# Eight chunks of the second feed-forward product as seven block products

## The chip, the cores and the metric

The kernel runs on one core of a Trainium2 chip, in one launch. The metric is device time in microseconds (us). The kernel before takes 1285.72 us, the median of three runs (1285.38 to 1285.79).

## The reference, cut to what matters

A trunk of four residual layers works on 256 tokens of 1024 channels, in float32. In each layer a token mixer is followed by a SwiGLU feed-forward block with 2816 hidden channels; only the second product of that block is touched here.

```
for i in range(4):
    x = x + concat([mix, mo]) @ w_o[i]                   # mixer and memory attention
    gu = rmsnorm(x, g_ffn[i]) @ w_ffn_in[i]              # 1024 -> 2 * 2816
    h = silu(gu[:, :2816]) * gu[:, 2816:]                # hidden, 256 x 2816
    x = x + h @ w_ffn_out[i]                             # 2816 -> 1024
out = rmsnorm(x, g_final)
```

## The kernel before, in words

All products run on TensorE (PE) in a reduced 32-bit form. Each operand is split into a high part and a low rest, and one 128 x 128 block of the left side meets 512 columns of the right in three matmuls: high by high, high by low, low by high (`mm3`, L136 to L138). A weight chunk comes by DMA from the SP queue into a tile `raw` (8 buffers); ScalarE (ACT) casts it to `whi` (L131) and VectorE (DVE) subtracts to get `wlo` (L132), 1024 elements per partition in one instruction. `whi` and `wlo` have 8 buffers each, so the splitting can run up to eight chunks ahead of PE.

`proj` forms 512 columns for two tiles of 128 tokens over the 1024 inputs. `strassen` forms 1024 columns (a left and a right half) in seven block products in place of eight: the tokens are halved (two tiles of 128), the inputs are halved (4 chunks of 128), the columns are halved. Each product has two steps `s` of two chunks, that is two times six matmuls (L214 to L216). The sums of weight blocks (`wsum`, and `raw` added in place; 8 adds of 1024 elements) are made on DVE at L224, and each of the 14 weight operands is split as any chunk is. The token sides are made once per layer by `tokens_side` (names `sh`, `sl`). The products share four PSUM banks: products 1 and 2; 5 and 3; 7 and 4; and 6. Between them stand `su = acc[6] + sv` and `sy = acc[7] + su` (L224): product 4 adds into the bank of product 7, so its first matmul waits until `sy` has read it. `strassen` is used before the change for column blocks b = 1 and b = 4 of the first feed-forward product; the use at b = 4 is called the first block product below.

The hidden values come out in six column blocks b (five of 512, one of 256). `h_out` or `gated` scales and gates them, and `hidden` transposes them on PE (L864), casts to `hh` on ACT (L867) and subtracts to `hl` on DVE (L868); block 5 uses one tile `hb`. These are the left sides of the second product.

`out_proj` forms that second product. It holds four PSUM banks (two token tiles by two column halves) over all 22 chunks of 128 hidden channels, 12 matmuls to a chunk; the last four chunks are held back and worked off bank by bank, so that the residual add (`residual`, L826), the transposes and the norm of the next layer start while PE still works.

The order of each engine's instructions is set by a scheduler when the kernel is built; each engine then takes its own list strictly in order. `later` and `flush` put off the transposes by some rounds. Tiles named `tag="att"` share 11 buffers, those of `big` share 12, and PSUM has 8 banks.

Of the kernel before, what the change touches and what calls it, by code (L numbers as in the profile page):

```python
# [9 lines left out]
F32 = mybir.dt.float32  # L10
F32R = mybir.dt.float32r
BF16 = mybir.dt.bfloat16
AF = mybir.ActivationFunctionType
ALU = mybir.AluOpType
# [3 lines left out]
P = 128  # L18
# [3 lines left out]
DEPTH = 4  # L22
# [4 lines left out]
NFF = DFF // P  # L27
# [5 lines left out]
NATT = 11  # L33


V_MIX, V_FFN, V_MEM, V_HEAD, V_CONV = 0, 32, 64, 72, 74
# [4 lines left out]
def trunk_kernel(ctx, tc, x, mem, vecs, w_in, w_kv, w_o, w_f1, w_f2, lams, g_final, out):  # L41
    nc = tc.nc
# [4 lines left out]
    big = pool("big", 12)  # L47
    xtp = pool("xtp", 2)
    work = pool("work", 2)
# [17 lines left out]
    xs = []  # L67
# [48 lines left out]
    def wchunk(srcs, nk, ncol, ahead=False):  # L116
        if ahead:
            raw = big.tile([P, nk, ncol], F32, name="raw", tag="big")
        else:
            raw = wraw.tile([P, nk, ncol], F32, name="raw", tag="raw")  # L120
        c = 0
        for s in srcs:
            n = s.shape[1]
            nc.sync.dma_start(raw[:, :, c:c + n], s.rearrange("(c p) n -> p c n", p=P))
            c += n
        return wparts(raw, nk, ncol)

    def wparts(raw, nk=2, ncol=512):
        hi = wsplit.tile([P, nk, ncol], F32R, name="whi", tag="whi")
        lo = wsplit.tile([P, nk, ncol], F32R, name="wlo", tag="wlo")  # L130
        nc.scalar.copy(hi, raw)  # L131
        wlast[:] = [nc.vector.tensor_tensor(lo, raw, hi.bitcast(F32), ALU.subtract)]  # L132
        return hi, lo

    def mm3(ps, lh, ll, wh, wl, first, last):
        nc.tensor.matmul(ps, lh, wh, start=first, stop=False)  # L136
        nc.tensor.matmul(ps, lh, wl, start=False, stop=False)  # L137
        return nc.tensor.matmul(ps, ll, wh, start=False, stop=last)  # L138
# [4 lines left out]
    def later(rounds, f):  # L143
        pend.append([rounds, f])
# [117 lines left out]
    def negative(rs):  # L262
# [3 lines left out]
            nc.vector.tensor_scalar(out[-1], r, -1.0, None, ALU.mult)  # L266
        return out

    def tokens_side(xg, xT):

        a11, a12, a21, a22 = xg[0][0], xg[0][1], xg[1][0], xg[1][1]
        half = lambda t, h: tuple(x[:, 4 * h:4 * h + 4, :] for x in xT[t])
        ab = {1: half(0, 0), 2: half(0, 1), 4: half(1, 1)}
        tt, stt = nc.vector.tensor_tensor, nc.vector.scalar_tensor_tensor

        def parts(src):
            hi = work.tile([P, 4, P], F32R, name="sh", tag="att", bufs=NATT)
            lo = work.tile([P, 4, P], F32R, name="sl", tag="att", bufs=NATT)
            nc.scalar.copy(hi, src)
            tt(lo, src, hi.bitcast(F32), ALU.subtract)  # L280
            return hi, lo

        tt(a22, a22, a21, ALU.subtract)
        ab[5] = parts(a22)
        tt(a21, a11, a21, ALU.subtract)
        ab[7] = parts(a21)
        stt(a11, a22, -1.0, a11, ALU.mult, ALU.subtract)
        ab[6] = parts(a11)
        stt(a12, a12, -1.0, a11, ALU.mult, ALU.subtract)
        ab[3] = parts(a12)  # L290
        return ab

    def out_proj(w, order, lhs, lag, evac, settle=None):

        acc = [[ps_acc.tile([P, 512], F32, name="acc", tag="ps") for _ in range(2)] for _ in range(NT)]
        chunks = [2 * kp + k for kp in order for k in range(2)]
        n = len(chunks)

        def mms(t, h, j, ch):
            lh, ll = lhs(chunks[j], t)  # L300
            sl = slice(h * 512, (h + 1) * 512)
            mm3(acc[t][h], lh, ll, ch[0][:, 0, sl], ch[1][:, 0, sl], j == 0, j == n - 1)

        tail = []
        for j, kc in enumerate(chunks):
            ch = wchunk([w[kc * P:(kc + 1) * P, :]], 1, D)
            if j < n - 2 * lag:
                for t in range(NT):
                    for h in range(2):
                        mms(t, h, j, ch)  # L310
                flush()
            else:
                tail.append((j, ch))
        if settle is not None:
            settle()
        for t in range(NT):
            for h in range(2):
                for j, ch in tail:
                    mms(t, h, j, ch)
                flush()  # L320
                evac(t, h, acc[t][h])
# [383 lines left out]
    for i in range(DEPTH):  # L705
# [117 lines left out]
        def residual(gcol, nxt, rnx, keep=None):  # L823
            def evac(t, h, acc):
                sl = slice(h * 512, (h + 1) * 512)
                nc.vector.tensor_tensor(xs[t][:, sl], acc, xs[t][:, sl], ALU.add)  # L826
                if h == 0:
                    nxt.append(xt_tiles())
                    if keep is not None:
                        keep.append([])  # L830
                later(1, lambda: transposed(nxt[t], xs[t], gcol, h, None if keep is None else keep[t]))
                if h == 1:
                    rnx.append(stats(xs[t]))
            return evac

        nxt, rnx, xg = [], [], []
# [2 lines left out]


        hts = []
        for b in range(6):
            n = 512 if b < 5 else 256
            if n == 512:
                hh = big.tile([P, 4, S], F32R, name="hh", tag="big")
                hl = big.tile([P, 4, S], F32R, name="hl", tag="big")
            else:
                both = big.tile([P, 2, 2, S], F32R, name="hb", tag="big")
                hh, hl = both[:, 0], both[:, 1]
            hts.append((hh, hl))  # L850
            sg = [work.tile([P, 512], F32, name="sg", tag="qkn", bufs=4) for _ in range(NT)]

            def h_out(t, g_ps, u_ps, hh=hh, hl=hl, sg=sg, n=n):
                s = sg[t][:, :n]
                if g_ps is not None:
                    nc.scalar.activation(s, g_ps, AF.Silu, scale=rx[t])
                if u_ps is not None:
                    nc.vector.scalar_tensor_tensor(s, u_ps, rx[t], s, ALU.mult, ALU.mult)
                    later(1, lambda: hidden(t, s, hh, hl, n))

            def hidden(t, s, hh, hl, n):
                tr = ps_x.tile([P, 4, P], F32, name="tr", tag="ps")
                for c in range(n // P):
                    nc.tensor.transpose(tr[:, c, :], s[:, c * P:(c + 1) * P], ident)  # L864
                src = tr[:, :n // P, :]
                hi = hh[:, :, t * P:(t + 1) * P]
                nc.scalar.copy(hi, src)  # L867
                nc.vector.tensor_tensor(hl[:, :, t * P:(t + 1) * P], src, hi.bitcast(F32), ALU.subtract)  # L868

            c0 = b * 512  # L870
            gcols, ucols = w_f1[i, :, c0:c0 + n], w_f1[i, :, DFF + c0:DFF + c0 + n]
            if b in (1, 4):
                def gated(t, side, ps, add, sg=sg, hh=hh, hl=hl, up={}):
                    if side == 0:
                        src = ps
                        if add is not None:
                            nc.vector.tensor_tensor(sg[t], ps, add, ALU.add)
                            src = sg[t]
                        nc.scalar.activation(sg[t], src, AF.Silu, scale=rx[t])
                        up[t, 0] = sg[t]  # L880
                    else:
                        up[t, 1] = add if t == 1 else work.tile([P, 512], F32, name="sx", tag="att", bufs=NATT)
                        nc.vector.tensor_tensor(up[t, 1], ps, add, ALU.add)
                    if (t, 0) in up and (t, 1) in up:
                        nc.vector.scalar_tensor_tensor(sg[t], up[t, 1], rneg[t], sg[t], ALU.mult, ALU.mult)
                        later(2, lambda: hidden(t, sg[t], hh, hl, 512))

                strassen(gcols, ucols, ab, gated)
            elif n == 512:
                proj([gcols], xT, lambda t, ps: h_out(t, ps, None))  # L890
                if b == 0:
                    ab, rneg = tokens_side(xg, xT), negative(rx)
                proj([ucols], xT, lambda t, ps: h_out(t, None, ps))
            else:
                proj([gcols, ucols], xT, lambda t, ps: h_out(t, ps[:, :n], ps[:, n:2 * n]))

        def f_lhs(kc, t):
# [2 lines left out]
            return hh[:, kc % 4, sl], hl[:, kc % 4, sl]  # L900

        nxt, rnx = [], []
        out_proj(w_f2[i], list(range(NFF // 2)), f_lhs, 2,
                 residual(V_MIX + 8 * (i + 1), nxt, rnx) if i + 1 < DEPTH else final())
        xT, rx = nxt, rnx


# [28 lines left out]
```

## Time and profile before

| | value |
|---|---|
| median of the runs | 1285.72 us |
| the profiled execution, its own time | 1284.95 us |
| its span | 1283.2 us |
| PE busy | 1270.3 us (99%) |
| DVE busy | 923.2 us (72%) |
| ACT busy | 721.4 us (56%) |

Some 1.7 us of the profiled execution lie outside its span. Busy time of PE is the union of matmuls whose ends are modelled, so a share of 99% says that matmuls follow each other without gaps, not that the array is at its peak. In a timeline row the first number is the start, the second the duration (of the whole group where xN is over 1), and the bracket at the end is the idle time of the engine just before it and what ended it. DVE and ACT instructions overlap a little at their ends: the price of one instruction in an unbroken run is the distance of two starts, not the duration. PEclk in the table of stages is the clock that TensorE was granted, as a share of 2.4 GHz.

### The profile page before, as it was taken

Reading aid. Unit: us, or ns where it says so; the run is one execution under the profiler, and the core shown is the slowest. Engines: PE = TensorE matmul, PEld = TensorE weight load, DVE = VectorE, ACT = ScalarE, POOL = GpSimd, SP = SyncE. Lnnn points to the kernel's source line nnn. Section 1 sums busy time; section 2 is a strip of 40 time slices with the busy share of each in tenths; the row PEclk is TensorE's granted clock in tenths of the full one; section 3 lists DMA queues with packets and bytes.
Section 4 is the critical chain, followed back from the end, with each engine's and each line's share of the span. In section 5 each row is a group of like instructions: output and inputs, shape, how many; then the busy total and the mean of one; then the engine's idle time right before and its main releaser. Section 6 shows DMA issues by size and latency. Waiting matters only on the chain.

```text
span 1283.2 us, 16324 instructions
## 1 busy us (share of the span) xinstructions
PE 1270.3 (99%) x6079; PEld 1046.2 (82%) x6079; DVE 923.2 (72%) x1147; ACT 721.4 (56%) x1015; POOL 55.0 (4%) x109
## 2 busy tenths in 40 slices
PE   9999999999999999999999999999999999999997
PEld 6888888878888888887888888887888888888786
DVE  7755599884566769988466778988646656998942
ACT  7756466564455646656355455656436755665642
POOL 1000000000111000000000000000000001000001
PEclk9999999999999999999999999999999999999999
DMA  9644438386554344848655553666765444383840
GB/s 347 199 145 134 145 115 279 116 290 206 149 184 131 132 148 122 272 131 291 191 158 164 173 190 105 200 202 200 244 195 165 132 132 148 103 279 110 270 156 33
DMA packets 107791, 227.34 MB, mean 177 GB/s; under 512 B 7488, under 2 KB 20288, under 8 KB 107712
## 3 DMA queue, kind: packets, MB, share of 16 engines
q1 hardware_dynamic: 107712, 226.31, 55.1%
q8 instruction: 47, 0.77, 0.2%
q14 instruction: 32, 0.26, 0.1%
HBM read 225.23 MB, written 1.05 MB: 176 GB/s over the span
## 4 chain that ended last, share of the span: by engine, by line
PE 91%; DVE 5%; ACT 1%; DMA 1%; issue 1%; SPq 0%; POOL 0%; POOLq 0%; ACTq 0%
PE acc L136 25%; PE acc L138 25%; PE acc L137 25%; PE acc L214 3%; DVE wlo L132 3%; PE acc L215 3%; PE acc L216 3%; PE tr L864 1%; PE tr L361 1%; PE tr L347 1%; DVE wsum L224 1%; ACT whi L131 1%; PE tr L430 1%; DMA raw<-in_w_ffn_out 1%; PE at L411 1%
## 5 line engine op out<-in xcount | busy, mean ns | idle before, releaser
L132 DVE TENSOR_TENSOR wlo<-raw,whi 128x1024 fp32r<-128x1024 f32 (+1 forms) x428 | 512.5, 1210 | 202.0 <-ACT whi L131 199.6
L131 ACT CAST whi<-raw 128x1024 fp32r<-128x1024 f32 (+1 forms) x428 | 438.8, 1042 | 291.0 <-PE acc L138 215.1
L136 PE MATMUL acc<-whi,xth 128*128 128x512 f32 (+1 forms) x896 | 353.5, 395 | 0.1
L137 PE MATMUL acc<-wlo,xth 128*128 128x512 f32 (+1 forms) x896 | 342.8, 383 | 1.6 <-DVE wlo L132 1.6
L138 PE MATMUL acc<-whi,xtl 128*128 128x512 f32 (+1 forms) x896 | 343.8, 384 | 0.0
L138 PEld LDWEIGHTS acc<-whi,xtl 128*128 128x128 f32 x896 | 168.4, 188 | 33.8
L137 PEld LDWEIGHTS acc<-wlo,xth 128*128 128x128 f32 x896 | 168.9, 188 | 32.6 <-DVE wlo L132 2.8
L136 PEld LDWEIGHTS acc<-whi,xth 128*128 128x128 f32 x896 | 168.6, 188 | 31.5 <-issue 0.8
L136 PE MATMUL acc<-whi,hh 128*128 128x512 f32 x320 | 125.4, 392 | 0.0
L138 PE MATMUL acc<-whi,hl 128*128 128x512 f32 x320 | 124.6, 389 | 0.0
L137 PE MATMUL acc<-wlo,hh 128*128 128x512 f32 x320 | 124.6, 389 | 0.0
L131 ACT CAST whi<-wsum 128x1024 fp32r<-128x1024 f32 x48 | 50.5, 1052 | 42.7 <-DVE wsum L224 39.2
L138 PEld LDWEIGHTS acc<-whi,hl 128*128 128x128 f32 x320 | 60.1, 188 | 12.6
L137 PEld LDWEIGHTS acc<-wlo,hh 128*128 128x128 f32 x320 | 60.1, 188 | 12.2
L136 PEld LDWEIGHTS acc<-whi,hh 128*128 128x128 f32 x320 | 60.1, 188 | 12.1
L132 DVE TENSOR_TENSOR wlo<-wsum,whi 128x1024 fp32r<-128x1024 f32 x48 | 58.4, 1217 | 5.8 <-ACT whi L131 5.2
L136 PE MATMUL acc<-whi,oh 128*128 128x512 f32 x128 | 51.1, 399 | 0.0
L214 PE MATMUL acc<-whi,sh 128*128 128x512 f32 x128 | 51.0, 399 | 0.0
L138 PE MATMUL acc<-whi,ol 128*128 128x512 f32 x128 | 50.0, 391 | 0.0
L216 PE MATMUL acc<-whi,sl 128*128 128x512 f32 x128 | 50.0, 390 | 0.0
L215 PE MATMUL acc<-wlo,sh 128*128 128x512 f32 x128 | 49.9, 390 | 0.0
L137 PE MATMUL acc<-wlo,oh 128*128 128x512 f32 x128 | 49.9, 390 | 0.0
(219 smaller groups left out, 1563.8 us busy)
## 6 DMA issues: line engine op xcount, KB each, us to landing
raw<-in_w_ffn_in SPq DMA_DIRECT2D x160, 512.0 KB, 4.5
raw<-in_w_in SPq DMA_DIRECT2D x100, 512.0 KB, 4.4
raw<-in_w_ffn_out SPq DMA_DIRECT2D x88, 512.0 KB, 4.6
raw<-in_w_o SPq DMA_DIRECT2D x40, 512.0 KB, 4.2
raw<-in_w_mem_kv SPq DMA_DIRECT2D x16, 512.0 KB, 4.4
raw<-in_w_ffn_in SPq DMA_DIRECT2D x32, 256.0 KB, 3.1
raw<-in_w_in SPq DMA_DIRECT2D x8, 256.0 KB, 5.6
x<-in_x SPq DMA_DIRECT2D x4, 256.0 KB, 4.2
```

The lines of the kernel that those rows point to most:

```text
L131: nc.scalar.copy(hi, raw)
L132: wlast[:] = [nc.vector.tensor_tensor(lo, raw, hi.bitcast(F32), ALU.subtract)]
L136: nc.tensor.matmul(ps, lh, wh, start=first, stop=False)
L137: nc.tensor.matmul(ps, lh, wl, start=False, stop=False)
L138: return nc.tensor.matmul(ps, ll, wh, start=False, stop=last)
L214: nc.tensor.matmul(acc[b], lh[:, kc, :], w[0][:, k, :], start=start, stop=False, skip_group_check=True)
L215: nc.tensor.matmul(acc[b], lh[:, kc, :], w[1][:, k, :], start=False, stop=False, skip_group_check=True)
L216: nc.tensor.matmul(acc[b], ll[:, kc, :], w[0][:, k, :], start=False, stop=stop, skip_group_check=True)
L224: nc.vector.tensor_tensor(out, a, b, ALU.add)
L347: last_pe = nc.tensor.transpose(ps[:, c, :], src[:, kc * P:(kc + 1) * P], ident).ins
L361: nc.tensor.transpose(ps[:, c, :], src[:, c * P:(c + 1) * P], ident)
L411: nc.tensor.matmul(pss[r][:, pr, :], qT[r * 64:(r + 1) * 64, a, pr, t * P:(t + 1) * P], kT[r * 64:(r + 1) * 64, b, pr, :], start=a + b == ...
```

## The change

Chunks 12 to 19 of the 22 (hidden blocks b = 3 and b = 4) leave the loop of `out_proj`. They are formed by `strassen` between the sixth and the seventh of the 14 chunks that remain; this is called the second block product below. The hidden side of its products is built in `hidden_side`, right after each transpose of b = 3 and b = 4, in one new tile `hsum` of `big` and eight tiles of `att`. Each finished quarter of the product is added to x at once in `quarter`, one or two adds of 512 elements, seven in all per layer; the rest of the product is added by `residual` as before. `token_parts` is `parts` of `tokens_side` under a new name.

```
-    def out_proj(w, order, lhs, lag, evac, settle=None):
+    def out_proj(w, order, lhs, lag, evac, settle=None, between=None):
         ...
         for j, kc in enumerate(chunks):
+            if between is not None and j == between[0]:
+                between[1]()
             ch = wchunk([w[kc * P:(kc + 1) * P, :]], 1, D)
...
+        def hidden_side(k, t, src):
+            tt, stt = nc.vector.tensor_tensor, nc.vector.scalar_tensor_tensor
+            if k == 0 and t == 0:
+                both = big.tile([P, 2, 4, P], F32, name="hsum", tag="big")
+                hsum["d"], hsum["a21"] = both[:, 0], both[:, 1]
+                nc.scalar.copy(hsum["d"], src)
+            elif k == 0:
+                nc.scalar.copy(hsum["a21"], src)
+                tt(hsum["d"], hsum["d"], src, ALU.subtract)
+                hab[7] = token_parts(hsum["d"])
+            elif t == 1:
+                tt(hsum["a21"], src, hsum["a21"], ALU.subtract)
+                hab[5] = token_parts(hsum["a21"])
+                stt(hsum["d"], hsum["d"], -1.0, src, ALU.mult, ALU.subtract)
+                hab[6] = token_parts(hsum["d"])
+            else:
+                stt(hsum["a21"], src, -1.0, hsum["d"], ALU.mult, ALU.subtract)
+                hab[3] = token_parts(hsum["a21"])
+                for p, g, t in ((1, 3, 0), (2, 4, 0), (4, 4, 1)):
+                    hab[p] = tuple(x[:, :, t * P:(t + 1) * P] for x in hts[g])
...
+                if b in (3, 4):
+                    hidden_side(b - 3, t, src)
...
+        def quarter(t, side, ps, add):
+            sl = slice(side * 512, (side + 1) * 512)
+            for part in (ps, add):
+                if part is not None:
+                    nc.vector.tensor_tensor(xs[t][:, sl], xs[t][:, sl], part, ALU.subtract if side else ALU.add)
+
+        def hidden_products():
+            w = w_f2[i, 12 * P:20 * P, :]
+            strassen(w[:, :512], w[:, 512:], hab, quarter)
+
-        out_proj(w_f2[i], list(range(NFF // 2)), f_lhs, 2,
-                 residual(V_MIX + 8 * (i + 1), nxt, rnx) if i + 1 < DEPTH else final())
+        out_proj(w_f2[i], [0, 1, 2, 3, 4, 5, 10], f_lhs, 2,
+                 residual(V_MIX + 8 * (i + 1), nxt, rnx) if i + 1 < DEPTH else final(),
+                 between=(6, hidden_products))
```

Three places show how the lists of DVE move. They are of layer 0; the numbers behind the names tell tiles apart, and lines above L266 are numbered anew (L224 and L132 keep theirs; L868 becomes L894, L883 becomes L911).

First, DVE near the end of the first block product, before the change: the split of product 4, step 0 (from `wsum_2339`) and of product 3, step 0 (from `raw_2326`), an add of weight blocks, and then the two sums `su` and `sy`.

```order
L132 TENSOR_TENSOR wlo_2464<-wsum_2339,whi_2463 128x1024
L132 TENSOR_TENSOR wlo_2474<-raw_2326,whi_2473 128x1024
L224 TENSOR_TENSOR wsum_2399<-wsum_2399,raw_2438 128x1024
L132 TENSOR_TENSOR wlo_2485<-wsum_2399,whi_2484 128x1024
L224 TENSOR_TENSOR su_2320<-acc_2376,sv_2319 128x512
L132 TENSOR_TENSOR wlo_2498<-raw_2387,whi_2497 128x1024
L224 TENSOR_TENSOR sy_2321<-acc_2364,su_2320 128x512
```

The same place on DVE after the change, with the first new instructions (L855, L273) in it.

```order
L855 TENSOR_TENSOR hsum_2302<-hsum_2302,tr_2354 128x512
L132 TENSOR_TENSOR wlo_2472<-wsum_2341,whi_2471 128x1024
L273 TENSOR_TENSOR sl_2364<-hsum_2302,sh_2363 128x512
L132 TENSOR_TENSOR wlo_2482<-raw_2328,whi_2481 128x1024
L224 TENSOR_TENSOR wsum_2407<-wsum_2407,raw_2446 128x1024
L224 TENSOR_TENSOR su_2322<-acc_2384,sv_2321 128x512
L224 TENSOR_TENSOR sy_2323<-acc_2372,su_2322 128x512
L132 TENSOR_TENSOR wlo_2493<-wsum_2407,whi_2492 128x1024
L911 TENSOR_TENSOR sy_2323<-acc_2347,sy_2323 128x512
L132 TENSOR_TENSOR wlo_2506<-raw_2395,whi_2505 128x1024
```

Two instructions of 512 elements are new, and `su` and `sy` have moved ahead of the last two splits of the product.

Second, DVE after the change around column block 5, where the rest of `hidden_side` stands (L858, L860, L863 and three L273) among splits of the first chunks of `out_proj`.

```order
L132 TENSOR_TENSOR wlo_2644<-raw_2641,whi_2643 128x1024
L894 TENSOR_TENSOR hl_2318<-tr_2562,hh_2317 128x4x128
L858 TENSOR_TENSOR hsum_2302<-tr_2562,hsum_2302 128x512
L860 SCALAR_TENSOR_TENSOR hsum_2302<-hsum_2302,tr_2562 128x512
L884 SCALAR_TENSOR_TENSOR sg_2519<-acc_2549,rstd_1522,sg_2519 128x256
L273 TENSOR_TENSOR sl_2571<-hsum_2302,sh_2570 128x512
L894 TENSOR_TENSOR hl_2318<-tr_2591,hh_2317 128x4x128
L273 TENSOR_TENSOR sl_2576<-hsum_2302,sh_2575 128x512
L863 SCALAR_TENSOR_TENSOR hsum_2302<-tr_2591,hsum_2302 128x512
L132 TENSOR_TENSOR wlo_2667<-raw_2664,whi_2666 128x1024
L132 TENSOR_TENSOR wlo_2685<-raw_2682,whi_2684 128x1024
L273 TENSOR_TENSOR sl_2600<-hsum_2302,sh_2599 128x512
```

Before the change only splits, two `hl`, one `sg` and nothing of L273 stand in this stretch.

Third, DVE after the change near the end of the second block product: splits for product 2, step 1 (`wlo_2879`), for 4 and 3, step 0 (`wlo_2893`, `wlo_2903`), the sums, the first adds to x (L936), and the splits for 4 and 3, step 1.

```order
L132 TENSOR_TENSOR wlo_2879<-raw_2866,whi_2878 128x1024
L132 TENSOR_TENSOR wlo_2893<-wsum_2774,whi_2892 128x1024
L936 TENSOR_TENSOR x1_169<-x1_169,acc_2780 128x512
L132 TENSOR_TENSOR wlo_2903<-raw_2761,whi_2902 128x1024
L224 TENSOR_TENSOR su_2755<-acc_2804,sv_2754 128x512
L224 TENSOR_TENSOR wsum_2827<-wsum_2827,raw_2866 128x1024
L224 TENSOR_TENSOR sy_2756<-acc_2792,su_2755 128x512
L699 TENSOR_SCALAR lam_3138<-lam_3138 128x1
L936 TENSOR_TENSOR x0_90<-x0_90,acc_2767 128x512
L936 TENSOR_TENSOR x1_169<-x1_169,sy_2756 128x512
L132 TENSOR_TENSOR wlo_2914<-wsum_2827,whi_2913 128x1024
L132 TENSOR_TENSOR wlo_2926<-raw_2815,whi_2925 128x1024
```

Where these stand there was one split per chunk of 12 matmuls before, and nothing else.

## Rows read from the trace of the kernel before

**Rows 1.** The page's head: span, and busy time of TensorE.
```profile
span 1283.2 us, 16324 instructions
PE 1270.3 (99%) x6079; PEld 1046.2 (82%) x6079; DVE 923.2 (72%) x1147; ACT 721.4 (56%) x1015; POOL 55.0 (4%) x109
```

**Rows 2.** Waits of PE: total us, times, longest.
```profile
PE acc L214 <- DVE sy L224: 2.5, 4, 0.7
```

**Rows 3.** Timeline of PE, layer 0, first block product to chunk seven.
```profile
249.90 0.39 PE L214 MATMUL acc<-whi,xth 128*128 128x512 f32 x1
...
263.99 0.39 PE L136 MATMUL acc<-whi,xth 128*128 128x512 f32 x1
265.03 0.50 PE L214 MATMUL acc<-whi,xth 128*128 128x512 f32 x1 [0.65 <-DVE sy L224]
...
282.53 0.39 PE L136 MATMUL acc<-whi,hh 128*128 128x512 f32 x1
...
299.10 0.39 PE L136 MATMUL acc<-whi,hh 128*128 128x512 f32 x1
...
302.50 0.39 PE L136 MATMUL acc<-whi,hh 128*128 128x512 f32 x1
```

**Rows 4.** Timeline of PE, layer 1, the same places.
```profile
568.64 0.39 PE L214 MATMUL acc<-whi,xth 128*128 128x512 f32 x1
...
583.72 0.50 PE L214 MATMUL acc<-whi,xth 128*128 128x512 f32 x1 [0.61 <-DVE sy L224]
...
617.75 0.39 PE L136 MATMUL acc<-whi,hh 128*128 128x512 f32 x1
```

**Rows 5.** Stages of layer 0: length, busy us of each engine, PEclk, DMA.
```profile
249.90:269.40 19.50, 18.85 (x85) 15.25 (x84) 18.33 (x20) 14.32 (x16) 0.00 (x0) 1.00 0.74 236
299.10:337.10 38.00, 38.00 (x169) 31.48 (x168) 16.62 (x14) 13.70 (x13) 0.00 (x0) 1.00 0.67 198
```

**Rows 6.** Timeline of DVE, layer 0, from the first block product on.
```profile
255.03 0.68 DVE L868 TENSOR_TENSOR hl<-tr,hh 128x512 fp32r<-128x512 f32 x1
255.63 1.21 DVE L132 TENSOR_TENSOR wlo<-raw,whi 128x1024 fp32r<-128x1024 f32 x1
...
261.42 1.22 DVE L132 TENSOR_TENSOR wlo<-wsum,whi 128x1024 fp32r<-128x1024 f32 x1 [1.17 <-ACT whi L131]
262.56 0.68 DVE L224 TENSOR_TENSOR su<-acc,sv 128x512 f32<-128x512 f32 x1
263.17 1.21 DVE L132 TENSOR_TENSOR wlo<-raw,whi 128x1024 fp32r<-128x1024 f32 x1
264.30 0.68 DVE L224 TENSOR_TENSOR sy<-acc,su 128x512 f32<-128x512 f32 x1
...
266.63 3.48 DVE L132 TENSOR_TENSOR wlo<-raw,whi 128x1024 fp32r<-128x1024 f32 x3
...
272.59 0.75 DVE L885 SCALAR_TENSOR_TENSOR sg<-sy,rneg,sg 128x512 f32<-128x512 f32 x1
273.25 0.75 DVE L885 SCALAR_TENSOR_TENSOR sg<-sx,rneg,sg 128x512 f32<-128x512 f32 x1
...
277.04 0.49 DVE L858 SCALAR_TENSOR_TENSOR sg<-acc,rstd,sg 128x256 f32<-128x256 f32 x1 [0.18 <-ACT sg L856]
277.44 1.22 DVE L132 TENSOR_TENSOR wlo<-raw,whi 128x1024 fp32r<-128x1024 f32 x1
```

**Rows 7.** Timeline of ACT in the same stretch.
```profile
261.29 3.89 ACT L131 CAST whi<-raw 128x1024 fp32r<-128x1024 f32 x4
```

**Rows 8.** The parameters of layer 1's attention, tile lamt: time to landing; timelines of POOL and DVE.
```profile
DMA to landing us min/median/max: 4.2/4.4/4.5
...
293.02 0.80 POOL L692 TENSOR_TENSOR lamt<-lamt 128x128 f32<-128x128 f32 x1 [1.77 <-DMA lamt<-in_lams]
...
293.85 0.42 DVE L693 TENSOR_REDUCE ls<-lamt 128x2 f32<-128x256 f32 x1 [0.35 <-POOL lamt L692]
```

**Rows 9.** Timeline of DVE at the end of layer 0: the first residual add.
```profile
334.66 0.69 DVE L826 TENSOR_TENSOR x<-acc,x 128x512 f32<-128x512 f32 x1 [0.41 <-PE acc L138]
```

More of the change, by code (lines that the diff above doesn't have):

```diff
@@ L267, in negative, with token_parts @@
         return out
+    def token_parts(src):
+        hi = work.tile([P, 4, P], F32R, name="sh", tag="att", bufs=NATT)
+        lo = work.tile([P, 4, P], F32R, name="sl", tag="att", bufs=NATT)
+        nc.scalar.copy(hi, src)
+        nc.vector.tensor_tensor(lo, src, hi.bitcast(F32), ALU.subtract)
+        return hi, lo
     def tokens_side(xg, xT):
@@ L274, in tokens_side @@
         tt, stt = nc.vector.tensor_tensor, nc.vector.scalar_tensor_tensor
[L276 to L281, printed above, removed]
         tt(a22, a22, a21, ALU.subtract)
-        ab[5] = parts(a22)
+        ab[5] = token_parts(a22)
         tt(a21, a11, a21, ALU.subtract)
-        ab[7] = parts(a21)
+        ab[7] = token_parts(a21)
         stt(a11, a22, -1.0, a11, ALU.mult, ALU.subtract)
-        ab[6] = parts(a11)
+        ab[6] = token_parts(a11)
         stt(a12, a12, -1.0, a11, ALU.mult, ALU.subtract)
-        ab[3] = parts(a12)
+        ab[3] = token_parts(a12)
         return ab
-    def out_proj(w, order, lhs, lag, evac, settle=None):
+    def out_proj(w, order, lhs, lag, evac, settle=None, between=None):
         acc = [[ps_acc.tile([P, 512], F32, name="acc", tag="ps") for _ in range(2)] for _ in range(NT)]
@@ L841, in trunk_kernel @@
         hts = []
+        hab, hsum = {}, {}
+        def hidden_side(k, t, src):
[18 more added lines that the diff above has]
+                    hab[p] = tuple(x[:, :, t * P:(t + 1) * P] for x in hts[g])
         for b in range(6):
@@ L851, in trunk_kernel, with h_out @@
             sg = [work.tile([P, 512], F32, name="sg", tag="qkn", bufs=4) for _ in range(NT)]
-            def h_out(t, g_ps, u_ps, hh=hh, hl=hl, sg=sg, n=n):
+            def h_out(t, g_ps, u_ps, hh=hh, hl=hl, sg=sg, n=n, b=b):
                 s = sg[t][:, :n]
@@ L858, in h_out, with hidden @@
                     nc.vector.scalar_tensor_tensor(s, u_ps, rx[t], s, ALU.mult, ALU.mult)
-                    later(1, lambda: hidden(t, s, hh, hl, n))
-            def hidden(t, s, hh, hl, n):
+                    later(1, lambda: hidden(t, s, hh, hl, n, b))
+            def hidden(t, s, hh, hl, n, b):
                 tr = ps_x.tile([P, 4, P], F32, name="tr", tag="ps")
@@ L872, in trunk_kernel, with gated @@
             if b in (1, 4):
-                def gated(t, side, ps, add, sg=sg, hh=hh, hl=hl, up={}):
+                def gated(t, side, ps, add, sg=sg, hh=hh, hl=hl, b=b, up={}):
                     if side == 0:
@@ L885, in gated @@
                         nc.vector.scalar_tensor_tensor(sg[t], up[t, 1], rneg[t], sg[t], ALU.mult, ALU.mult)
-                        later(2, lambda: hidden(t, sg[t], hh, hl, 512))
+                        later(2, lambda: hidden(t, sg[t], hh, hl, 512, b))
                 strassen(gcols, ucols, ab, gated)
```

## The prediction, made before the changed kernel was run

> **What bounds the kernel now.** I read the page's head first, then the waits of PE, then its timeline through the feed-forward block, and last the timelines of DVE and ACT beside it. The head shows PE busy 99% of the span [rows 1], and the waits leave it hardly a pause: the only one that comes back is four waits of product 4 in a block product for `sy`, 2.5 us in all [rows 2]. So time is the number of matmuls by their distance. From 299.10 to 302.50 PE starts 15 matmuls of 512 columns: 0.2267 us each [rows 3]. A change that takes matmuls away pays this per matmul as long as DVE and ACT deliver. Their headroom is local: in `out_proj` DVE is busy 16.6 of 38.0 us, in a block product 18.3 of 19.5 [rows 5]. A block product is therefore fed from the lead built up in the eight split buffers before it, and the question is whether that lead lasts for two of them with only 30 us between.
>
> **Matmuls.** Eight chunks take 8 x 12 = 96 matmuls, seven products take 7 x 12 = 84. Twelve go per layer, 48 in all: 48 x 0.2267 = 10.9 us less. All were on the path. No transposes are added, the DMA bytes are the same (eight loads of 512 KB either way).
>
> **The old wait for `sy`.** In layer 0 PE starts the last matmul before product 4 at 263.99 and product 4 at 265.03, 0.81 us later than the usual distance [rows 3]; DVE began `sy` at 264.30, after a split that starts at 263.17 and after 1.17 us of waiting for ACT's cast [rows 6]. Layer 1 shows the same wait [rows 4], and four are counted [rows 2], so 3.2 us hang on it. The new list puts `su` and `sy` ahead of that split and fills the wait for the cast with them. Summed from `hl` at 255.03 with the prices below: three splits and two adds of 512, then the third split and the add of weight blocks end near 261.4, `su` and `sy` near 262.7. PE wants them at 264.0. I take the wait as gone: -3.2 us; the other end is that it stays, 0. The first matmul of product 3 needs L911's read of its bank at about 265.5 and gets it near 264.4.
>
> **What DVE gets.** Prices are distances of starts in an unbroken run: 1.135 us for 1024 elements (three splits in 3.48 us with 1.22 for the last), 0.60 for 512 (`su` to the next), 0.66 for a scalar_tensor_tensor of 512, 0.40 for 256 [rows 6]. The second block product needs 14 splits and 8 adds of weight blocks where 8 splits stood (+14 x 1.135 = 15.9 us), `su` and `sy` (1.2), seven adds to x (4.2), and `hidden_side` brings six instructions of 0.60 and two of 0.66 (4.9): 26 us more per layer, some 105 us over the four. DVE's 28% of idle time covers that as a sum. What counts is the moment, so I add up the new list from the last `hl` before the new work, which starts 5.1 us after the first block product's start in layer 0 (255.03 against 249.90), to the `sy` of the second: 36 x 1.135 + 17 x 0.60 + 4 x 0.66 + 4 x 0.40 = 55.3 us, so 60.4 us after that start if DVE never waits. In the old list such a stretch holds idle times of 1.17 and 0.18 for ACT [rows 6] and two more of that kind; the first is filled now. Walking the new list against the transposes and gates it must wait for in column block 5, I get 1.2 us of waits (some 0.2 at each of six places). `sy` is then ready 61.6 us after the start.
>
> PE wants it later: it starts the seventh chunk at 299.10 now, at 298.3 without the old wait, and product 4 comes 61 matmuls (13.8 us) later: 62.2 us after its start at 249.90. Layer 1 gives the same, 617.75 - 568.64 - 0.8 + 13.8 = 62.1 [rows 4]. So the margin is 0.5 us. In layer 0 the reduction for lambda (0.42 [rows 8]) and a smaller instruction stand in this stretch too, and take the margin. Behind `sy` come two adds to x and the splits for step 1 of products 4 and 3, each about half a microsecond ahead of PE, then one split per 2.72 us, where DVE gains again. DVE being late is paid once, since these points share one queue. From below the wait can be 0; from above I let DVE's waits double and add a microsecond, 1.9 us a layer. I take 0.4 a layer, +1.6 us, near the lower end because the sum itself says no wait.
>
> **Other edits.** ACT gets six more casts of weights a layer, six copies and casts of 512 in `hidden_side`, and `sv`; four casts take 3.89 us [rows 7], and it is busy 14.3 of 19.5 us in a block product against DVE's 18.3 [rows 5], so DVE decides. `lamt` moves on SP to between the third and fourth load of the second block product, behind the release of `hsum`, its new buffer. That is near 282.4; the landing takes 4.4 us, the POOL products 1.3, and DVE's reduction [rows 8] comes near 289.4, just when the chain is ready. If it is late, DVE, which takes its list in order, stands still with all later splits behind it; up to 1.5 us once, in layer 0. `gfin` moves likewise in layer 3, where nothing waits for it. The adds to x run in `out_proj`; at its end the residual add waits for PE today [rows 9], and after the change DVE is back at that point about when PE is.
>
> **Sum.** -10.9 - 3.2 + 1.6 = -12.5 us against the profiled execution of 1284.95 us (span 1283.2 and some 1.7 around it): 1272.5. That execution stands 0.8 us under the median of the runs, 1285.72; from the median the sum gives 1273.2, which I forecast.
>
> **A rule that speaks against it.** DVE instructions start 0.08 to 0.09 us before the drawn end of the one in front: 1.22 long, 1.135 apart [rows 6]. The Trainium skill ("VectorE: DVE Perf Modes", section "The DRAIN you can't avoid") says that the next instruction doesn't start until the pipeline of the one before has emptied. Read on durations, its sum would be rival C's below, 1290; here the trace disagrees, since starts lie closer than the durations (the section itself adds that an instruction that isn't held starts earlier).
>
> **Rivals.**
> A. DVE is late in every layer by the upper bound, and a wait of 1.9 us for `sy` or a split opens in the second block product: -14.1 + 7.6 = -6.5, 1279.2. For it speaks the margin of half a microsecond after 60 instructions, against it the idle time of ACT. Chance 0.16.
> B. The old wait for `sy` stays because `hidden_side` pushes the add of weight blocks back by as much as the reordering wins: -10.9 + 1.6 = -9.3, 1276.4. Against it speaks 1.3 us of room. Chance 0.08.
> C. The other side: DVE's queue does not overlap its instructions through this mix of PSUM and SBUF sources and pays durations, 1.22, 0.68 and 0.75 [rows 6]: 36 x 0.085 + 17 x 0.08 + 4 x 0.09 + 0.3 = 5.1 us more, `sy` at 66.7 against 62.2, and 4.5 us of wait per layer: -14.1 + 18 = +4, 1290. It decides from 3.5 us per layer (14.1 / 4) on. Against it speak the starts just named. Chance 0.03.
> D. The freed time does not show, because PE then waits elsewhere in the layer for what it has caught up with (weight loads, the residual adds): between 1283 and 1288. DVE idles more than half of the stage behind [rows 5], so 0.03.
>
> **How the numbers follow.** The forecast holds 0.70. Its own bounds are no wait at all, -14.1 (1271.6), and the upper end for half of the layers; A and B lie inside a range of 1270.8 to 1279, with C and D outside. This kernel can tell a difference of about 0.2%, 2.6 us, from none: the forecast, A and B are all beyond it on the fast side, 0.94; D is mostly within, 0.03; C is slower, 0.03.
>
> **What will show it.** PE's matmuls at L214 to L216 should rise by 336 (4 x 84), and those at L136 to L138 with `hh` fall by 384 (4 x 96). The waits of PE should have lost the four of `sy` in the first block product, and show at most four of a few tenths in the second, on `sy` or on the split for product 4, step 1. DVE should run unbroken from the first block product to the end of the second. In layer 0 a DVE idle time ended by POOL would show `lamt` late. I am wrong if PE waits over 2 us in each second block product, or if granted clock or matmul distance changes.

## The result, and the profile after

The changed kernel takes 1271.69 us, the median of four runs (1271.41 to 1272.02), against 1285.72 us before, also the median of four: a ratio of 0.9891, with a 95% interval of 0.9874 to 0.9909. That is 14.0 us less; 1273.2 was forecast. The profiled span goes from 1283.2 us [rows 1] to 1269.7, 13.5 us less. The head of the page after:

```profile
span 1269.7 us, 16380 instructions
PE 1258.3 (99%) x6031; PEld 1036.9 (82%) x6031; DVE 1022.4 (81%) x1271; ACT 753.3 (59%) x1067; POOL 55.7 (4%) x109
```

PE has 48 matmuls less, DVE 99 us more work, ACT 32 us more. Two rows of the table of groups (out<-in, shapes, count, busy us and mean ns, idle before), both of high matmuls, show the exchange: `sh` at L214 had 128 before and `hh` at L136 320. With 48 of `hh` at L214, where none stood, and three matmuls to each high one, L214 to L216 rise by 336 and `hh` at L136 to L138 falls by 384, as forecast.

```profile
L214 PE MATMUL acc<-whi,sh 128*128 128x512 f32 x192 | 75.9, 396 | 0.0
L136 PE MATMUL acc<-whi,hh 128*128 128x512 f32 x192 | 75.6, 394 | 0.0
```

The waits of PE (total us, times, longest), against [rows 2]:

```profile
PE acc L136 <- ACT xth L356: 1.1, 1, 1.1
...
PE acc L214 <- DVE lam L699: 0.2, 1, 0.2
```

The four waits for `sy` are gone. One small wait is listed at L214, in layer 0. The row of `xth`, and three waits for `wlo` at L137, are of the first 15 us of the kernel, ahead of all that the change touches. The timeline of PE shows where time left and came back. Layer 0 first, in the places of [rows 3], then layer 1, as [rows 4]; each row begins with start and duration:

```profile
250.01 0.39 PE L214 MATMUL acc<-whi,xth 128*128 128x512 f32 x1
...
263.86 0.39 PE L216 MATMUL acc<-whi,xtl 128*128 128x512 f32 x1
264.08 0.39 PE L214 MATMUL acc<-whi,xth 128*128 128x512 f32 x1
...
281.62 0.39 PE L136 MATMUL acc<-whi,hh 128*128 128x512 f32 x1
...
298.19 0.39 PE L214 MATMUL acc<-whi,hh 128*128 128x512 f32 x1
...
311.79 0.39 PE L214 MATMUL acc<-whi,sh 128*128 128x512 f32 x1
312.40 0.51 PE L214 MATMUL acc<-whi,hh 128*128 128x512 f32 x1 [0.22 <-DVE lam L699]
...
317.79 0.39 PE L136 MATMUL acc<-whi,hh 128*128 128x512 f32 x1
...
565.52 0.39 PE L214 MATMUL acc<-whi,xth 128*128 128x512 f32 x1
...
613.74 0.39 PE L214 MATMUL acc<-whi,hh 128*128 128x512 f32 x1
...
627.11 0.39 PE L216 MATMUL acc<-whi,hl 128*128 128x512 f32 x1
627.37 0.50 PE L214 MATMUL acc<-whi,hh 128*128 128x512 f32 x1
...
632.94 0.39 PE L136 MATMUL acc<-whi,hh 128*128 128x512 f32 x1
```

At 264.08 product 4 of the first block product follows at the usual distance, 0.22 us; before it stood 1.04 us behind [rows 3]. From the start of that product to the first matmul of `out_proj` it is 31.61 us (281.62 - 250.01), where it was 32.63 [rows 3]: 1.02 us less, and 0.90, 0.92 and 0.92 in the other layers. The second block product should take 84 x 0.2268 = 19.05 us; it takes 19.60 in layer 0 (317.79 - 298.19) and 19.20 in layer 1 (632.94 - 613.74), 19.23 and 19.20 in the last two: 0.55, 0.15, 0.18 and 0.15 more. In layers 1 to 3 PE just misses `sy`: the matmul at 627.37 starts 0.26 us after the one in front, which the list of waits doesn't show. The book of the span, then: matmuls -10.88, first block product -3.76, second +1.03, and 0.11 more in all that stands ahead of the first block product of layer 0: -13.50 us, as measured.

DVE in the same stretch of layer 0, and its `sy` of layer 1:

```profile
261.63 0.69 DVE L224 TENSOR_TENSOR su<-acc,sv 128x512 f32<-128x512 f32 x1
262.36 0.69 DVE L224 TENSOR_TENSOR sy<-acc,su 128x512 f32<-128x512 f32 x1
...
289.45 0.41 DVE L695 TENSOR_REDUCE ls<-lamt 128x2 f32<-128x256 f32 x1
...
311.66 0.68 DVE L224 TENSOR_TENSOR sy<-acc,su 128x512 f32<-128x512 f32 x1
...
331.82 0.68 DVE L828 TENSOR_TENSOR x<-acc,x 128x512 f32<-128x512 f32 x1
...
626.62 0.69 DVE L224 TENSOR_TENSOR sy<-acc,su 128x512 f32<-128x512 f32 x1
```

`sy` of the first block product now begins at 262.36, where it began at 264.30 [rows 6]. The reduction for lambda stands at 289.45 with no wait in front of it. In layer 1 `sy` of the second block product ends at 627.31, where PE is ready. And the stage of the second block product in layer 0, with length, busy us of PE, PEld, DVE, ACT and POOL, clock, DMA share and GB/s:

```profile
298.19:317.79 19.60, 19.38 (x86) 15.69 (x84) 19.60 (x22) 12.34 (x14) 0.00 (x0) 1.00 0.63 186
```

DVE is busy 19.60 of 19.60 us there, at the full granted clock. It has no reserve left, and yet PE loses only some tenths.

### The profile page after: what moved, and what is told of

The parts are those of the page before. It is cut to its first block, busy times and chain, and to the rows that moved or that the text cites. A ratio compares the mean times of both kernels' runs of the same rounds, so it can differ in the third digit from the quotient of the medians.

```text
span 1269.7 us, 16380 instructions
## 1 busy us (share of the span) xinstructions
PE 1258.3 (99%) x6031; PEld 1036.9 (82%) x6031; DVE 1022.4 (81%) x1271; ACT 753.3 (59%) x1067; POOL 55.7 (4%) x109
## 4 chain that ended last, share of the span: by engine, by line
PE 95%; DVE 2%; ACT 1%; issue 1%; DMA 0%; SPq 0%; POOL 0%; POOLq 0%; ACTq 0%
PE acc L136 23%; PE acc L138 23%; PE acc L137 23%; PE acc L214 6%; PE acc L216 6%; PE acc L215 6%; PE tr L890 2%; PE tr L363 1%; DVE wlo L132 1%; PE tr L349 1%; PE tr L432 1%; PE at L413 1%; PE at L445 1%; PE at L479 1%; PE at L521 1%; DVE wsum L224 1%
## 5 line engine op out<-in xcount | busy, mean ns | idle before, releaser
L132 DVE TENSOR_TENSOR wlo<-raw,whi 128x1024 fp32r<-128x1024 f32 (+1 forms) x428 | 508.0, 1210 | 101.3 <-ACT whi L131 99.0
L131 ACT CAST whi<-raw 128x1024 fp32r<-128x1024 f32 (+1 forms) x428 | 434.1, 1041 | 198.8 <-PE acc L138 122.6
L136 PE MATMUL acc<-whi,xth 128*128 128x512 f32 (+1 forms) x896 | 353.6, 395 | 1.1 <-ACT xth L356 1.1
L137 PE MATMUL acc<-wlo,xth 128*128 128x512 f32 (+1 forms) x896 | 342.9, 383 | 1.3 <-DVE wlo L132 1.3
L138 PE MATMUL acc<-whi,xtl 128*128 128x512 f32 (+1 forms) x896 | 343.9, 384 | 0.0
L138 PEld LDWEIGHTS acc<-whi,xtl 128*128 128x128 f32 x896 | 168.4, 188 | 33.8
L137 PEld LDWEIGHTS acc<-wlo,xth 128*128 128x128 f32 x896 | 168.9, 189 | 32.3 <-DVE wlo L132 2.5
L136 PEld LDWEIGHTS acc<-whi,xth 128*128 128x128 f32 x896 | 168.7, 188 | 32.5 <-ACT xth L356 1.6
L131 ACT CAST whi<-wsum 128x1024 fp32r<-128x1024 f32 x72 | 75.7, 1052 | 85.4 <-DVE wsum L224 81.5
L132 DVE TENSOR_TENSOR wlo<-wsum,whi 128x1024 fp32r<-128x1024 f32 x72 | 87.7, 1218 | 1.5 <-ACT whi L131 0.7
L214 PE MATMUL acc<-whi,sh 128*128 128x512 f32 x192 | 75.9, 396 | 0.0
L136 PE MATMUL acc<-whi,hh 128*128 128x512 f32 x192 | 75.6, 394 | 0.0
L216 PE MATMUL acc<-whi,sl 128*128 128x512 f32 x192 | 74.9, 390 | 0.0
L138 PE MATMUL acc<-whi,hl 128*128 128x512 f32 x192 | 74.8, 390 | 0.0
L137 PE MATMUL acc<-wlo,hh 128*128 128x512 f32 x192 | 74.8, 390 | 0.0
L224 DVE TENSOR_TENSOR wsum<-wsum,raw 128x1024 f32<-128x1024 f32 x48 | 57.8, 1218 | 0.3
L136 PE MATMUL acc<-whi,oh 128*128 128x512 f32 x128 | 51.1, 400 | 0.0
L138 PE MATMUL acc<-whi,ol 128*128 128x512 f32 x128 | 50.0, 391 | 0.0
L137 PE MATMUL acc<-wlo,oh 128*128 128x512 f32 x128 | 49.9, 390 | 0.0
L214 PEld LDWEIGHTS acc<-whi,sh 128*128 128x128 f32 x192 | 36.1, 188 | 8.2 <-DVE sy L911 1.1
L216 PEld LDWEIGHTS acc<-whi,sl 128*128 128x128 f32 x192 | 36.1, 188 | 7.7
```

The source lines that it names most:

```text
L214: nc.tensor.matmul(acc[b], lh[:, kc, :], w[0][:, k, :], start=start, stop=False, skip_group_check=True)
L216: nc.tensor.matmul(acc[b], ll[:, kc, :], w[0][:, k, :], start=False, stop=stop, skip_group_check=True)
L224: nc.vector.tensor_tensor(out, a, b, ALU.add)
```

## Experiments

Each kernel was timed in five rounds against the kernel before. Line numbers of an edited kernel can stand a few lines off the changed kernel's.

**The hidden side alone.** The sums of hidden values are made and thrown away; `out_proj` takes all 22 chunks as before the change.

```
-                 residual(...) ..., between=(6, hidden_products))
+        out_proj(w_f2[i], list(range(NFF // 2)), f_lhs, 2, residual(...) ...)
```

> The kernel before with hidden_side added and its results unused: all 22 chunks stay in out_proj, no second block product. Theory: the wait for sy in the first block product goes because the new instructions move su and sy ahead of a split in DVE's list; PE loses nothing elsewhere, so 1285.7 - 3.8 = 1281.9, no wait of L214 left. Rival 1: the wait went because of the second block product or the fewer matmuls; then it stays here, 1285.7. Rival 2: 4.9 us more DVE work per layer costs PE time by itself; over 1286.

Measured: 1282.15 us (1281.42 to 1284.18) against 1285.49, ratio 0.9974 (0.9964 to 0.9983). The waits of PE hold no row of L214 and no `sy` any more; the largest that is left:

```profile
PE acc L137 <- DVE wlo L132: 1.5, 3, 0.8
```

So the new instructions of `hidden_side` take the old wait away by themselves, though they only add work to DVE and ACT: they re-sort the lists of both. And they cost PE nothing that the time shows.

**The products without the hidden side.** The second block product stays, but products 3, 5, 6 and 7 take hidden values as left sides in place of the sums (another result, the same matmuls).

```
-                if b in (3, 4):
-                    hidden_side(b - 3, t, src)
+            for p, g, t in (..., (7, 3, 1), (5, 4, 1), (6, 3, 0), (3, 4, 0)):
+                hab[p] = tuple(x[:, :, t * P:(t + 1) * P] for x in hts[g])
```

> The changed kernel without hidden_side: products 3, 5, 6 and 7 of the second block product take hidden values themselves as left sides in place of the sums, so that part of the computation is changed; matmuls, weights and adds to x are the same. DVE's list has su, a split, then sy in the first block product again. Theory: the four waits for sy come back there (+3.8) and the small loss in the second block product goes (-1.0), since DVE has 4.9 us less to do before it: 1274.5. Rival: the order of su and sy is not the cause and the wait stays away: 1270.7.

Measured: 1274.81 us (1274.62 to 1275.39), ratio 0.9918 (0.9904 to 0.9932). The old wait is back, with the sum of [rows 2]:

```profile
PE acc L214 <- DVE sy L224: 2.5, 4, 0.7
```

The second block product takes 19.07 to 19.08 us in every layer here, no loss. The parts of the book are thereby shown apart: the products alone give 10.7 us (1285.49 - 1274.81), near the 10.9 of the matmuls, and the changed kernel's other 3.1 (1274.81 - 1271.69) are near the old wait less what the second product loses (3.8 - 1.0 = 2.8).

**The second block product two chunks into `out_proj`, in place of six.** DVE then has four chunks less in which to build a lead.

```
-                 between=(6, hidden_products))
+                 between=(2, hidden_products))
```

> The changed kernel with the second block product after two chunks of out_proj in place of six; all counts are the same. Theory: what carries the second block product is the lead that DVE builds up over the chunks in front, 2.72 - 1.135 = 1.6 us per chunk; four chunks fewer take 6.3 us of it in each layer, none is to spare, and PE waits as long: 1271.7 + 25 = 1297, slower than the kernel before. Rival: the lead is in the eight split buffers anyway and the place does not matter: 1271.7.

Measured: 1297.10 us (1296.80 to 1297.49) against 1285.28, ratio 1.009 (1.0077 to 1.0104). The same work in another place is slower than before. The waits of PE:

```profile
PE acc L214 <- ACT whi L131: 10.8, 20, 0.8
...
PE acc L214 <- DVE x L936: 3.8, 4, 1.0
```

ACT is named with 10.8 us, but its casts of `wsum` wait for DVE's adds, as here in layer 1; the engine that is late is DVE.

```profile
624.96 1.04 ACT L131 CAST whi<-wsum 128x1024 fp32r<-128x1024 f32 x1 [3.92 <-DVE wsum L224]
```

The expected time, 1297, came from the lead alone, 6.3 us a layer. The second block product takes 25.70 to 26.18 us here, 6.5 to 6.6 more than in the changed kernel.

**One split more, and three more.** The first split of the second block product is made again on DVE, once or three times, which takes 1.135 us each from the lead.

```
+        for _ in range(again.pop() if again else 0):
+            nc.vector.tensor_tensor(lo, raw, hi.bitcast(F32), ALU.subtract)
```

Once:

> The changed kernel with the first split of the second block product made twice on DVE, 1.135 us more in each of the four layers. Theory: DVE runs unbroken up to sy and hands it over without room, so PE is later by the same amount in each layer: 1271.7 + 4.5 = 1276.2, with waits of L214 in the second block products of about 1.1 us each. Rival 1: there is still half a microsecond of room, as forecast: 1274.2. Rival 2: DVE is not what limits this stretch: 1271.7.

Measured: 1273.02 us (1272.60 to 1273.85), ratio 0.9904 (0.9891 to 0.9918). My main theory fell: 1.3 us over the changed kernel, where 4.5 was expected. DVE, then PE, in layer 1 (in this run and the next the cast of L131 stands at L132, and what stood at L132 and after it three lines further on):

```profile
628.21 0.68 DVE L227 TENSOR_TENSOR sy<-acc,su 128x512 f32<-128x512 f32 x1
```
```profile
628.72 0.39 PE L217 MATMUL acc<-whi,sh 128*128 128x512 f32 x1
628.95 0.49 PE L217 MATMUL acc<-whi,hh 128*128 128x512 f32 x1
```

`sy` comes 1.6 us later than in the changed kernel, at 628.89, but four matmuls of product 3 (the last at 628.72) now stand in PE's list ahead of product 4, which starts at 628.95, in time. The extra instruction had moved PE's list as well. How much of the 1.3 us is load and how much is the new order isn't separated. Three times:

> As the run before with the split made four times, 3.4 us more of DVE in each layer. Theory without room: 1271.7 + 13.6 = 1285.3, the whole gain gone. With half a microsecond of room: 1283.3. If DVE does not limit the stretch: 1271.7.

Measured: 1286.88 us (1285.98 to 1289.59), ratio 1.0012 (1.0003 to 1.0021). That is 15.2 us over the changed kernel, 3.8 a layer for 3.4 us of added DVE work. PE in layer 1:

```profile
634.85 0.50 PE L218 MATMUL acc<-wlo,sh 128*128 128x512 f32 x1 [0.90 <-DVE wlo L135]
```

PE now waits four times in this product, twice for `wlo` and twice for `whi`, behind the added splits. So the lead is indeed all but used up in the changed kernel: the two splits that this run has more than the last add 2.3 us of DVE work a layer and cost 3.5 ((1286.88 - 1273.02) / 4). Why the price is above the work isn't shown; the lists differ here too.

**`sy` ahead of an add of weight blocks.** The add `wsum + b21` of step 1 of the second block product stands ahead of `sy` in the changed kernel; here it is held until `sy` has been issued. No work is added or removed.

```
+            if second and s == 1:
+                with tc.issue_after(ysum.ins):
+                    plus(sums[s], sums[s], b21[s])
```

> The changed kernel with one add of weight blocks in the second block product (wsum + b21, step 1) held until sy is issued; DVE's work is the same, sy comes 1.1 us earlier. Theory: the small loss in the second block product (0.55 us in layer 0, 0.15 to 0.18 in the others) is a wait for sy as it stands in the list, and the split for product 4, step 1, which is now later, still comes in time: 1271.7 - 1.0 = 1270.7. Rival: DVE as a whole is late, so the wait only moves to that split: 1271.7.

Measured: 1271.00 us (1270.81 to 1271.20) against 1285.28, ratio 0.9888 (0.9873 to 0.9903). DVE, then PE, in layer 1:

```profile
625.48 0.69 DVE L224 TENSOR_TENSOR sy<-acc,su 128x512 f32<-128x512 f32 x1
```
```profile
626.98 0.39 PE L216 MATMUL acc<-whi,hl 128*128 128x512 f32 x1
627.21 0.39 PE L214 MATMUL acc<-whi,hh 128*128 128x512 f32 x1
```

`sy` is 1.1 us earlier and product 4 follows at 0.23 us. The second block product takes 19.03 to 19.04 us in layers 1 to 3, so its gaps are gone there. In layer 0 it still takes 19.35: the split for product 4, step 1, now behind `sy` and the adds to x, comes late. PE in layer 0:

```profile
315.02 0.50 PE L215 MATMUL acc<-wlo,hh 128*128 128x512 f32 x1
```

This start stands 0.41 us behind the one in front (314.61), in place of 0.23. So in layer 0 the rival, that the wait moves to that split, is right for half of the loss. A second pair of runs on one chip gave 1270.91 (1270.58 to 1271.14) for this kernel and 1271.81 (1271.56 to 1271.89) for the changed one, 0.9 us apart without overlap of the ranges:

> The changed kernel with the add of weight blocks held behind sy in the second block product, again: 0.6 to 0.7 us less than the run before, 1270.8, if the small waits for sy were what was left of the loss; equal to it if the difference lay between chips.

> The changed kernel again, beside the next run on the same chip: 1271.5.

This version beats both kernels. Of the 1.0 us that the second block product had lost it gets 0.8 back in PE's rows (0.25, 0.16, 0.19 and 0.17), and 0.7 and 0.9 in the times of the two pairs.

**Eight chunks ahead in place of six.** If the missing lead were the cause, two chunks more should have helped as well.

```
-                 between=(6, hidden_products))
+                 between=(8, hidden_products))
```

> The changed kernel with the second block product after eight chunks in place of six. Theory: 3.2 us more lead in each layer; no waits in the second block product, 1270.7. Rival: DVE's list has a split between su and sy again here, and a wait as in the kernel before comes back in each layer: 1274.5.

Measured: 1271.59 us (1271.44 to 1272.06), ratio 0.9892 (0.9879 to 0.9906): no gain, and not the full old wait either, which the rival expected. DVE, then PE, in layer 1:

```profile
631.50 1.22 DVE L132 TENSOR_TENSOR wlo<-raw,whi 128x1024 fp32r<-128x1024 f32 x1
632.63 0.68 DVE L224 TENSOR_TENSOR sy<-acc,su 128x512 f32<-128x512 f32 x1
```
```profile
633.04 0.39 PE L216 MATMUL acc<-whi,sl 128*128 128x512 f32 x1
633.37 0.50 PE L214 MATMUL acc<-whi,hh 128*128 128x512 f32 x1
```

The new list has a split between `su` and `sy`, and PE gets to product 4 as `sy` ends (633.31). DVE also stands idle twice in this product, 1.20 and 0.57 us, for ACT's casts of `wsum`, which themselves wait for DVE's adds; in the changed kernel it has no idle time there. So some of the two chunks' lead was there, and DVE spent it standing idle. With the run before, I read this so that the last tenths hang on the order of the list, and the lead decides only whether they are tenths; in this run the two aren't separated, since its list differs too.

**Low parts on POOL.** Three of the four subtractions at L273 go to POOL, which is idle there.

```
-                hab[5] = token_parts(hsum["a21"])
+                hab[5] = token_parts(hsum["a21"], nc.gpsimd)      # likewise hab[6], hab[3]
```

> The changed kernel with three of the four low parts of the hidden sums (products 5, 6 and 3) subtracted on POOL in place of DVE: 1.8 us less on DVE per layer before the second block product. Theory: the loss there goes, 1270.7. Rival 1: the splits on POOL are late and product 5 waits for them: over 1273. Rival 2: POOL's work slows DVE's instructions beside it: 1271.7 or more.

Measured: 1278.77 us (1278.74 to 1279.16), ratio 0.9949 (0.9936 to 0.9961), 7.1 us over the changed kernel. The theory fell. The waits of PE that are new, then POOL and DVE in layer 1:

```profile
PE tr L890 <- DVE sg L884: 3.7, 4, 0.9
PE acc L214 <- DVE sy L224: 2.7, 4, 1.3
```
```profile
594.28 2.22 POOL L273 TENSOR_TENSOR sl<-hsum,sh 128x512 fp32r<-128x512 f32 x1 [110.68 <-ACT sh L272]
...
598.13 1.87 POOL L273 TENSOR_TENSOR sl<-hsum,sh 128x512 fp32r<-128x512 f32 x1 [0.36 <-ACT sh L272]
```
```profile
596.54 0.69 DVE L863 SCALAR_TENSOR_TENSOR hsum<-tr,hsum 128x512 f32<-128x512 f32 x1 [0.59 <-POOL sl L273]
...
598.77 2.31 DVE L132 TENSOR_TENSOR wlo<-raw,whi 128x1024 fp32r<-128x1024 f32 x1
```

POOL takes 1.8 us on average for what DVE does in 0.68, and DVE's split beside it 2.31 in place of 1.22. DVE also waits for POOL, which still reads the tile that L863 overwrites. DVE's gate of column block 5 (L884) and its `sy` come later for it, and PE waits for both in each layer; no product waits for the splits on POOL themselves, so it is the second rival that came true. The Trainium skill ("Perfetto Trace Analysis", section "Optimizing Scalar/DVE Operations") says that the two share a read port of SBUF, so that moving work between them might not help. The trace agrees, with 1.1 us added to that split and 7.1 to the kernel; that the port is the cause isn't shown.

**The old list with `sy` first.** In the kernel before, the split that stood ahead of `sy` in a block product is held until `sy` has been issued.

```
+        with tc.issue_after(hold) if hold is not None else ExitStack():
             wlast[:] = [nc.vector.tensor_tensor(lo, raw, hi.bitcast(F32), ALU.subtract)]
```

> The kernel before with one edit: in a block product the last split but one (product 4, step 1) is held until sy is issued, so that su and sy stand ahead of it in DVE's list, without any new work. Theory: 3.8 us of the change's gain is this order alone, 1285.5 - 3.8 = 1281.7, no wait for sy left. Rival: the new instructions of hidden_side were needed too, since they filled DVE's wait for a cast; then about half stays, 1283.6.

Measured: 1284.38 us (1283.27 to 1286.14) against 1285.47, ratio 0.9991 (0.9982 to 1.0). The runs spread widely, and the interval reaches no gain at all; the theory's 1281.7 lies outside it, the rival's 1283.6 inside. The wait for `sy` is gone, and another stands in its place, in each layer:

```profile
PE tr L865 <- DVE sg L886: 2.4, 4, 0.8
```

ACT, then DVE, then PE in layer 1 show how it comes about. The first row of PE is the start of the first block product:

```profile
589.83 1.06 ACT L131 CAST whi<-raw 128x1024 fp32r<-128x1024 f32 x1 [1.13 <-DMA raw<-in_w_ffn_out]
590.79 0.71 ACT L880 ACTIVATE sg<-sg,rstd 128x512 f32<-128x512 f32 x1
```
```profile
591.54 0.75 DVE L886 SCALAR_TENSOR_TENSOR sg<-sy,rneg,sg 128x512 f32<-128x512 f32 x1 [0.79 <-ACT sg L880]
```
```profile
569.08 0.39 PE L215 MATMUL acc<-whi,xth 128*128 128x512 f32 x1
...
592.44 0.63 PE L865 MATMUL tr<-ident,sg 128*128 128x128 f32 x4 [0.71 <-DVE sg L886]
```

The same activation in the kernel before, and in the changed kernel:

```profile
590.45 0.72 ACT L879 ACTIVATE sg<-sg,rstd 128x512 f32<-128x512 f32 x1
```
```profile
586.24 0.71 ACT L907 ACTIVATE sg<-sg,rstd 128x512 f32<-128x512 f32 x1
```

ACT's list is the same here as in the kernel before: the activation stands behind a cast that waits for its load, and comes 21.7 us after the start of the block product (21.3 to 21.8 in the other layers), where it came after 21.8 in the kernel before (590.45 - 568.64 [rows 4]; 21.8 to 21.9 in the others). The gate on DVE waits for it, and PE, which is now earlier, waits for the gate with its transposes. In the changed kernel one cast less stands ahead of the activation, two in layer 3, and in every layer it comes 20.7 us after the start (586.24 - 565.52). So the 3.8 us came with the re-sorted lists of both DVE and ACT, not with the order of `sy` alone.

## Why the prediction was right

**Matmuls, -10.9: as forecast.** 48 fewer matmuls on the head, distance and clock unchanged, and 1274.81 us for the products alone, 10.7 under the kernel before in that series.

**The old wait, -3.2: it went, and was worth 3.8.** The step that `su` and `sy` fill DVE's wait for the cast was right: they start at 261.63 and 262.36, end near 263.05 (forecast 262.7), and PE comes at 264.08. The size was short by 0.5 because only the distance to the first matmul behind the wait was counted. After such a pause PE starts the next ones too slowly: behind the wait at 312.40 in layer 0 of the changed kernel the next starts are 0.34, 0.24 and 0.24 us apart. But that the whole wait turned into time was in part luck. The prediction looked at DVE's list and took ACT's not to matter; the old list with `sy` first shows that PE then stops a little later, for a gate that waits for ACT's activation, and that the median falls by only 1.1 us. In the changed list that activation has moved ahead too, by 1.1 us, which the prediction didn't look at. Rival B, that the wait stays, is excluded by the row at 264.08 and by the hidden side alone.

**The second block product, +1.6: +1.0.** `sy` of layer 1 was forecast 61.6 us after the start of the first block product and ended 61.8 after it (626.62 + 0.69 - 565.52); PE was forecast to want it at 62.1 and was there at 61.8. The margin of 0.5 was none: 0.2 went on DVE's side, 0.1 because PE gained 0.9 and not 0.8 in front, and 0.2 because product 4 comes 60 matmuls after the start there (13.6 us), not 61 as in layer 0, from whose list I had counted. A miss by hundredths costs 0.15 us a layer, less than the 0.4 taken. In layer 0 the two small instructions for lambda took more, as said: 0.55 us, of which 0.22 is idle; the profile names `lam`, which stands right behind `sy` in DVE's list. That the lead carries the product is shown by the two-chunk run, whose price was expected at 25 us and came to 25.4; that the rest hangs on `sy` in layers 1 to 3, and not on DVE's total or on a split, by `sy` first, which gets 0.7 to 0.9 us back with all the work in place. In layer 0, with lambda's instructions, DVE's total is short as well: the split behind `sy` is late there.

**`lamt`, up to 1.5 once: nothing.** The reduction came at 289.45, forecast 289.4, and DVE didn't wait for it.

**DVE's prices.** Busy time rose by 99 us, some 105 were forecast. In the second block product DVE runs unbroken at distances of 1.135 us. Rival C, durations in place of distances, would have meant waits of 4.5 us a layer; there are none. Rival A asked for 1.9 us a layer, and the most is 0.55. Rival D, that PE would wait elsewhere for what it had caught up with, has no row of waits to stand on here: of the 14.6 us taken away all but 1.1 shows in the span. Its mechanism is real, though: it is what the old list with `sy` first ran into. At the end of the layer DVE is back at the residual add at 331.82, with no wait, as forecast.

**Not foreseen:** a wait of 1.1 us for `xth` at the start of the kernel, ahead of all that the change touches. All that stands ahead of the first block product grew by only 0.1 us, so it cost no more than that; it differs from kernel to kernel (none to 1.3 us), and isn't explained.

## What to carry to other kernels

Fewer matmuls are worth their full distance only while the engine that feeds them has a lead: count the lead in us at the start of the dense stage and the price of every instruction to its end, as distances of starts; the same product four chunks earlier turned a gain of 14 us into a loss of nearly 12. An instruction that is added can re-sort the lists of all engines, so read the new lists, and not only that of the engine it was added to, before giving it a price: added work alone won 3.3 us here, and putting the right instruction first in one engine's old list won 1.1 at the median, not clear of none, of the 3.8 that were to be had, since another engine's list held the next wait.

## What the runs showed of the hardware

POOL and DVE slow each other on two-input work: the twelve subtractions of 512 columns on POOL take 1.30 to 2.22 us, 1.8 on average, where DVE takes 0.68, and a split of DVE beside one takes 2.31 in place of 1.22 (the rows of 598.13 and 598.77 above). The changed kernel shows it too, where POOL multiplies for lambda: DVE's add of weight blocks beside it takes 1.48 us.

```profile
287.64 0.81 POOL L694 TENSOR_TENSOR lamt<-lamt 128x128 f32<-128x128 f32 x1 [0.59 <-DMA lamt<-in_lams]
```
```profile
288.05 1.48 DVE L224 TENSOR_TENSOR wsum<-raw 128x1024 f32<-128x1024 f32 x1
```

And a short wait of PE costs more than its idle time. The one at 312.40 has 0.22 us of idle time, and the second block product is 0.55 longer. The matmul in front is drawn 0.39 long, where the next one otherwise starts 0.23 behind it, so 0.16 of the delay doesn't count as idle; the rest lies in the matmuls behind, which start 0.34, 0.24 and 0.24 us apart, at a granted clock that stays 1.00.
